# Input projections of a two-layer hybrid block: when weights, masks, decays and latents are queued

## Chip, core and metric

One core of a Trainium2 chip runs the whole program. The metric is the device time of one execution in microseconds (us); of several runs the median is taken. Five engines work side by side, each through its own list of instructions: TensorE (PE in the profile, with its weight loads as PEld), VectorE (DVE), ScalarE (ACT), GpSimd (POOL) and SyncE (SP), which in this kernel issues every DMA.

## What is computed

1024 latent tokens and 256 context tokens, each of 1024 features, pass through two layers. A layer normalises its input, projects it with one wide matrix into the columns of four head groups, runs each group, gates the results, and adds one output projection to the stream. The reference, cut to the projections and the parts that the change touches:

```python
def hybrid_layer(x, xc, ...):
    h = rmsnorm(x, norm_w) * (1 + scale[:, None]) + shift[:, None]
    hc = rmsnorm(xc, norm_w) * (1 + scale_c) + shift_c
    pl = split_cols(h @ w_in, IN_WIDTHS)        # A: cq, ckv, kr, gate; B, C: q, k, v, gate; D: z, xbc, dt
    pc = split_cols(hc @ w_in, IN_WIDTHS)
    ya_l, ya_c = mla_branch(...)                # A
    ...
    x = x + gate[:, None] * (jnp.concatenate([ya_l, yb_l, yc_l, yd_l], axis=-1) @ w_out)

def mla_keys(ckv, k_rope, kv_norm_w, w_kv_up, rope):
    kv = (rmsnorm(ckv, kv_norm_w) @ w_kv_up).reshape(bsz, n, MLA_HEADS, MLA_NOPE + MLA_V)
    ...
def mla_queries(cq, q_norm_w, w_q_up, rope):
    q = (rmsnorm(cq, q_norm_w) @ w_q_up).reshape(bsz, n, MLA_HEADS, MLA_NOPE + MLA_ROPE)
    ...
def ssd_scan(x, dt, bm, cm, a, init, with_output):
    a_cum = jnp.cumsum((dt * a).reshape(bsz, nc, SSD_CHUNK, nh), axis=2)   # the decays
    ...
```

Group A expands a latent of 128 features (`ckv`) to keys and values with `w_kv_up`, and one of 256 features (`cq`) to queries with `w_q_up`. Group D needs running sums of `dt * a` along the tokens, its decays. The second layer computes no output for context tokens.

## The kernel before

Every large product is made in float32r from a split of both factors into a high and a low half: three matmuls (L128, L129, L130: high by high, low weight by high, high by low) for each one of the reference. A weight tile arrives as `..._raw`, ACT casts it to the high half (L291) and DVE subtracts to get the low half (L292). This is `split_w`, L286. `split` (L282 to L284) does the same for an activation.

Buffers: `bg` is a ring of six tiles of 128x1024 words, for raw weights, splits on their way to DRAM (`qkhl`, `chl`, `ka`, `qa`) and latents on their way back (`c`); `tm` is a ring of eight. There are 35 general slots (`Slot`), taken and given back by hand in the program. Products of two kinds and all transpositions use the PSUM ring `TR` of two.

A layer first runs `in_proj`, then attention, then the output projection. `in_proj` is a list of 22 jobs, numbered 0 to 21. Job 0 makes the rotary key and the `dt` columns; after its last token group `after_decays` (L809) turns `dt` into decays: `Ssd.decays` is a chain of some thirty small steps on 128x80 tiles on DVE and ACT, three matmuls (two matmul instructions each in the profile) of `dta` with triangles of ones and with ones (`ps_cum`, L447 to L449), and more small steps on the result. Jobs 1 to 6 are the convolved columns, 7 to 12 gates, 13 and 14 `cq`, 15 `ckv`, 16 to 19 the token-major columns (`tm`) of groups B and C, and 20 and 21 the last two gates. A job fetches the next job's weights as it starts (`fetch`, L613).

The token-major jobs walk through tokens in pairs of tiles. The third step of a pair transposes (`ps_qkt`, L781) and sends the split result off (`qkhl`, L784, L785, L787). During jobs 17 to 19 each pair also takes two steps from the list `up`, made by `up_steps` (L832), which is group A's expansion: `begin` loads and splits both up-projection weights (`wqu`, 512 KB; `wku`, 256 KB); `load` and `load_q` fetch latents `c` (L846), which `norm` had stored; `keys` (`ps_k`), `values` (`ps_v`) and `queries` (`ps_q`) are products; `end` gives back slots. Three token groups are gone through (256 context tokens, then 512 and 512 latent ones); `AHEAD` says how many steps ahead of the end of the list so far a latent's load is put in. What is left of the list is run as job 20 starts (L1024 and after). At 2 steps a pair, layer 0 takes 30 steps inside the jobs and layer 1 takes 28.

The order of the work is set in two ways. In attention, PE's order is written out by hand (`manual_schedule`). Elsewhere the framework orders each engine's instructions as it builds the program: of those that its own timing takes to be ready, the one that stands first in the program. `soon` is a list of [delay, function]; `flush` (L795) calls, after each product group, what has come due, and `issue_after` keeps it behind that group's last matmul on PE. SP runs its DMAs in the order that it was given, and waits in front of one whose source or buffer isn't ready.

Attention's first pair of heads is prepared in the last two jobs. `first` is a list of steps (loads of `kk`, `qq`, scores `ps_s`, maxima `mp` at L1148, then `row`, the step that sends the row of maxima through `ps_m`, `ng` and a DMA to `ql`), filled with `idle` steps at its end (L1357). They are dealt out evenly over job 21's units (eight to each token group: 24 in layer 0 and 16 in layer 1).

Masks: `mask_r` (L152 to L158) holds 128x640 words of constants from DRAM, cast to float32r, and the identity; the scan of group D and the row step use it. The prologue (L1480 to L1529) loads and normalises the tokens and makes the modulation vectors.

Of the kernel before, what the change touches and what calls it, by code (L numbers as in the profile page):

```python
# [9 lines left out]
F32 = mybir.dt.float32  # L10
# [7 lines left out]
P = 128  # L18
# [16 lines left out]
POOL_TM = ()  # L35
UP_RATE = {17: 2, 18: 2, 19: 2}
SCALE_V = True
AHEAD = 1
SIDE0, SIDE1 = 2, 7
MAKE_AT = (1, 0)  # L40
THIRD = 3
# [16 lines left out]
def hybrid_block(ctx, tc, x, ctxt, c_t, w_fm, w_tm, w_mod, b_gate, p_col, p_row, w_qu, w_kvu, w_out,  # L58
# [49 lines left out]
    def free_all(slots):  # L108
        for s in slots:
            s.free()  # L110
# [13 lines left out]
    def ps(tag, name=None):  # L124
        return pp.tile([P, 512], F32, tag=tag, bufs=PS_BUFS[tag], name=name or f"ps_{tag}")
# [6 lines left out]
    def f32(ap):  # L132
        return ap.bitcast(F32)
# [15 lines left out]
    nc.sync.dma_start(out=base, in_=consts[:, 0:4 * P])  # L149
    ident, tri_u, tri_l, ones = [base[:, i * P:(i + 1) * P] for i in range(4)]  # L150
    rtm, cs = const([P, 8, 96]), const([P, 8, 32])
    mask_f = bg(name="mask_f")  # L152
    nc.sync.dma_start(out=mask_f[:, 0:5 * P], in_=consts[:, 4 * P:])
    mask_r = cp.tile([P, 6 * P], F32R, name="mask_r")
    nc.vector.tensor_copy(mask_r[:, 0:5 * P], mask_f[:, 0:5 * P])
    nc.vector.tensor_copy(mask_r[:, 5 * P:6 * P], ident)
    ident_r = mask_r[:, 5 * P:6 * P]
    st_r = [mask_r[:, 3 * P:4 * P], mask_r[:, 4 * P:5 * P]]  # L158
    mhalf = const([P, 16])
# [122 lines left out]
    def split(dst_hi, dst_lo, src, eng):  # L282
        nc.scalar.copy(dst_hi, src)  # L283
        eng.tensor_tensor(out=dst_lo, in0=src, in1=f32(dst_hi), op=ALU.subtract)  # L284

    def split_w(src, name, n=1024, eng=None):  # L286
        raw = bg((P, n), name=name + "_raw")
        nc.sync.dma_start(out=raw, in_=src)
        hi = Slot([P, n], F32R, name + "_hi")
        lo = Slot([P, n], F32R, name + "_lo")  # L290
        nc.scalar.copy(hi.t, raw)  # L291
        (eng or nc.vector).tensor_tensor(out=lo.t, in0=raw, in1=f32(hi.t), op=ALU.subtract)  # L292
        return hi, lo


# [117 lines left out]
    class Ssd:  # L413
# [5 lines left out]
        def decays(self, dt_raw):  # L419
# [24 lines left out]
            nc.vector.tensor_scalar(out=am, in0=am, scalar1=-1.0, scalar2=None, op0=ALU.mult)  # L444
            dta, acum, tot, dec = v, e1, e2, e3
            nc.vector.tensor_tensor(out=dta, in0=dt, in1=am.unsqueeze(1).to_broadcast(S80), op=ALU.mult)
            pcum = ps("TR", name="ps_cum")  # L447
            for i, tri in enumerate((tri_u, tri_l, ones)):
                mm(pcum[:, i * 80:i * 80 + 80], lhsT=tri, rhs=dta.rearrange("p t c -> p (t c)"), start=True, stop=True)  # L449
# [8 lines left out]
            nc.vector.tensor_tensor(out=dec, in0=dec, in1=dt, op=ALU.mult)  # L458
            self.dta = [acum.bitcast(F32R), dta.bitcast(F32R)]
            split(*self.dta, dta, nc.vector)  # L460
            self.dt, self.eac, self.etot, self.dec = dt, eac, etot, dec

        def alloc_y(self):
            (self.y, self.y_slots) = toks(["yd0", "yd1"], F32, self.need_ctx)
# [148 lines left out]
    def fetch(L, j):  # L613
        if j[0] == "tm":
            br, half = j[1]
            return [split_w(w_tm[L, br, half, :, u, :], f"wtm{u}", eng=nc.gpsimd if (br * 2 + half, u) in POOL_TM else None)
                    for u in range(2)]
        return [split_w(w_fm[L, j[1]], "wfm", eng=nc.gpsimd if j[1] in POOL_FM else None)]

    def products(ht, w, lo, n, tag="MX", each=lambda: None, ks=range(8), p=None):  # L620
        hh, hl, _ = ht
# [9 lines left out]
    def in_proj(L, ht, need_ctx, side, follow, both, begun, make_last):  # L631
# [177 lines left out]
        def after_decays():  # L809
            ssd.decays(dt_raw)  # L810
            free_all(dt_slots)

        def start_ssd():
            ssd.alloc_y()
# [17 lines left out]
        def up_steps():  # L832
            W = {}

            def begin():
                rf.append(load_rope_fm())
                W["q"] = split_w(w_qu[L], "wqu")
                raw = bg((P, 512), name="wku_raw")
                nc.sync.dma_start(out=raw, in_=w_kvu[L])
                W["ks"] = Slot([P, 2, 512], F32R, "wku")  # L840
                W["k"] = [W["ks"].t[:, e, :] for e in range(2)]
                split(*W["k"], raw, nc.vector)

            def latent(i, lo, n):
                r = bg((P, 2, 512), F32R, name="c")
# [3 lines left out]
            def load(lo, n):  # L849
                W["ck", lo] = latent(2, lo, n)  # L850
# [47 lines left out]
                W["ks"].free()  # L898
                rf.pop().free()

            r = [begin]
            for lo, n in GROUPS:
                r.insert(-AHEAD if lo else len(r), lambda lo=lo, n=n: load(lo, n))
                r += [lambda pair=pair, lo=lo, n=n: keys(pair, lo, n) for pair in range(2)]
                r += [lambda lo=lo, t=t: values(lo, t) for t in range(lo // P, (lo + n) // P, 2)]
                if lo >= NCTX or need_ctx:
                    r.insert(-1, lambda lo=lo, n=n: load_q(lo, n))
                    r += [lambda h=h, lo=lo, n=n: queries(h, lo, n) for h in range(4)]
            return r + [end]

# [127 lines left out]
    def attention(L, res, need_ctx, y, late, ahead):  # L1038
# [315 lines left out]
            return r + more, row  # L1354

        first, row = prep(*pairs[0])
        yield first + [row] + [idle] * 4  # L1357
        y_slots, tail = [], []
        order_of_pe = ExitStack()
        order_of_pe.enter_context(tc.manual_schedule(engines={mybir.EngineType.PE}))  # L1360
# [145 lines left out]
    for part in range(4):  # L1506
        if part == X_AT:
            load_x(range(6, NTILE))
        for i in range(4):
            if part and i >= AFTER:  # L1510
                for _ in range(-(-len(due) // (5 - i))):
                    due.pop(0)()
            mod_a[4 * part + i]()
        if part == X_AT:
            for t in range(6, NTILE):
                x_hat(xs[t].t)
            raw.update(early_ht(xs, GROUPS[2:]))
        if part % 2 == 0:
            add_half(ht)
        last, due = due, []  # L1520
        for g in ready:
            made(g, part)
        for f in last:
            f()
        if part == X_AT:
            for p in range(part + 1):
                made(GROUPS[2], p)
            ready.append(GROUPS[2])
    nc.sync.dma_start(out=rtm, in_=rope_tm)  # L1529
    for L in range(DEPTH):  # L1530
        need_ctx = L < DEPTH - 1
# [139 lines left out]
```

## Time and profile before

| | |
|---|---|
| median of 3 runs | 1789.11 us (1788.35 to 1792.08) |
| profiled execution, own time | 1792.62 us |
| its span (first to last instruction) | 1790.8 us |
| mean granted TensorE clock over the span | 0.990 |
| PE busy | 1713.7 us (96%) |
| DVE busy | 1137.0 us (63%) |
| POOL busy | 786.8 us (44%) |
| ACT busy | 731.3 us (41%) |
| DMA queue's share of 16 engines | 41.2% |

The profiled execution is one run of its own, 3.5 us above the median. Its rows are in microseconds from the span's start. "Granted clock" is the share of TensorE's full clock that the chip gave it in a stretch. In the timeline a bracket shows how long the engine had been idle before the instruction, and what released it; `x2` joins like instructions that follow one another. Matmuls overlap, so a start-to-start distance tells more than one's length.

### The profile page before, as it was taken

What the parts mean: (1) busy time and instruction counts of PE and PEld (TensorE: products, weight loads), DVE (VectorE), ACT (ScalarE), POOL (GpSimd) and SP (SyncE); (2) the same over time, 40 slices, a digit from 0 to 9 for tenths busy, and PEclk for the clock granted to TensorE, in tenths of its full rate; (3) what the DMA queues carried; (4) which work ended last, traced back from release to release, by engine and by line L of the source; (5) the groups of instructions that cost most, each with busy time, mean ns of one, the idle gap of its engine ahead of it and who ended that gap; (6) DMA issues with size and microseconds to landing.
All of it is one profiled execution on the core that took longest, in us unless ns stands there. A gap on an engine that the chain in (4) does not pass through costs nothing.

```text
span 1790.8 us, 27801 instructions
## 1 busy us (share of the span) xinstructions
PE 1713.7 (96%) x9658; PEld 1334.7 (75%) x9658; DVE 1137.0 (63%) x2291; ACT 731.3 (41%) x2049; POOL 786.8 (44%) x735
## 2 busy tenths in 40 slices
PE   6999999999989999999999899999999999999998
PEld 4677888889976566666787678888898655666686
DVE  6877864374347766577645797762743776657753
ACT  5433433333224555556424333343322355554531
POOL 2423642042325766656323234531332377666622
PEclk9999999999999999999999999999999999999999
DMA  9474323165556431431511344241568643131521
GB/s 321 143 239 150 116 101 127 60 203 192 194 157 173 115 98 31 114 102 63 194 59 42 111 151 148 75 144 60 182 196 249 176 131 91 32 92 60 160 69 56
DMA packets 130480, 231.61 MB, mean 129 GB/s; under 512 B 13826, under 2 KB 74628, under 8 KB 130340
## 3 DMA queue, kind: packets, MB, share of 16 engines
q1 hardware_dynamic: 130340, 229.84, 41.2%
q8 instruction: 76, 1.25, 0.3%
q14 instruction: 64, 0.52, 0.1%
HBM read 161.23 MB, written 68.45 MB: 128 GB/s over the span
## 4 chain that ended last, share of the span: by engine, by line
PE 52%; DVE 11%; DMA 4%; POOL 2%; issue 2%; ACT 2%; SPq 0%; POOLq 0%; DVEq 0%; ACTq 0%
PE ps_acc L1239 8%; PE ps_s L1144 4%; PE ps_fm L129 3%; PE ps_fm L130 3%; PE ps_fm L128 3%; PE ps_o L130 3%; PE ps_o L128 3%; PE ps_o L129 3%; PE ps_st L1227 3%; PE ps_st L1230 2%; PE ps_st L1222 2%; DVE mp L1148 2%; PE ps_st L1223 2%; PE ps_st L1224 2%; PE ps_tm L128 1%
## 5 line engine op out<-in xcount | busy, mean ns | idle before, releaser
L1254 POOL TENSOR_TENSOR ac<-ac,P 128x512 f32<-128x512 f32 (+3 forms) x248 | 308.2, 1261 | 130.6 <-ACT P L1231 95.4
L1231 ACT ACTIVATE P<-ps_st 128x512 f32<-128x512 f32 (+3 forms) x456 | 243.3, 553 | 214.3 <-PE ps_st L1230 98.5
L1148 DVE TENSOR_REDUCE mp<-ps_s 128x1 f32<-128x512 f32 (+3 forms) x428 | 259.2, 656 | 100.8 <-PE ps_s L1144 96.3
L128 PE MATMUL ps_fm<-hh,wfm_hi 128*128 128x512 f32 x576 | 234.2, 407 | 2.6 <-DVE kb L660 1.9
L130 PE MATMUL ps_fm<-hl,wfm_hi 128*128 128x512 f32 x576 | 232.2, 403 | 2.2 <-POOL hl L405 1.0
L129 PE MATMUL ps_fm<-hh,wfm_lo 128*128 128x512 f32 x576 | 230.1, 399 | 0.0
L128 PE MATMUL ps_tm<-wtm_hi,hh 128*128 128x256 f32 x512 | 147.1, 287 | 1.6 <-ACT ka L283 1.6
L129 PE MATMUL ps_tm<-wtm_hi,hl 128*128 128x256 f32 x512 | 146.2, 286 | 0.0
L130 PE MATMUL ps_tm<-wtm_lo,hh 128*128 128x256 f32 x512 | 146.2, 286 | 0.0
L1254 DVE TENSOR_TENSOR ac<-ac,P 128x512 f32<-128x512 f32 (+3 forms) x88 | 98.7, 1121 | 53.5 <-ACT P L1231 19.5
L130 PEld LDWEIGHTS ps_fm<-hl,wfm_hi 128*128 128x128 f32 x576 | 109.5, 190 | 28.9 <-POOL hl L405 4.5
L128 PEld LDWEIGHTS ps_fm<-hh,wfm_hi 128*128 128x128 f32 x576 | 109.8, 191 | 27.5 <-issue 5.1
L129 PEld LDWEIGHTS ps_fm<-hh,wfm_lo 128*128 128x128 f32 x576 | 109.7, 190 | 21.4 <-issue 2.5
L1248 POOL TENSOR_TENSOR ac<-P 128x1024 f32<-128x1024 f32 (+1 forms) x30 | 65.9, 2198 | 117.1 <-ACT P L1231 99.7
L128 PE MATMUL ps_o<-wo_hi,yh 128*128 128x512 f32 x288 | 112.6, 392 | 1.4 <-ACT yh L1403 1.3
L129 PE MATMUL ps_o<-wo_hi,yl 128*128 128x512 f32 x288 | 112.1, 390 | 1.4 <-DVE yl L1404 1.4
L130 PE MATMUL ps_o<-wo_lo,yh 128*128 128x512 f32 x288 | 112.0, 390 | 0.0
L128 PEld LDWEIGHTS ps_tm<-wtm_hi,hh 128*128 128x128 f32 x512 | 99.1, 194 | 3.9 <-ACT ka L283 2.0
L130 PEld LDWEIGHTS ps_tm<-wtm_lo,hh 128*128 128x128 f32 x512 | 99.3, 194 | 0.6 <-issue 0.4
L129 PEld LDWEIGHTS ps_tm<-wtm_hi,hl 128*128 128x128 f32 x512 | 99.2, 194 | 0.5
L1448 POOL TENSOR_TENSOR xres<-xres,dl 128x512 f32<-128x512 f32 x32 | 42.4, 1326 | 95.6 <-DVE dl L1447 92.4
L1239 PE MATMUL ps_acc<-P,vt 128*64 128x512 f32 (+3 forms) x416 | 82.5, 525 | 0.0
(342 smaller groups left out, 4123.9 us busy)
## 6 DMA issues: line engine op xcount, KB each, us to landing
wfm_raw<-in_w_fm_dram SPq DMA_DIRECT2D x36, 512.0 KB
wm<-in_w_mod_dram SPq DMA_DIRECT2D x64, 256.0 KB
d_q<-qkhl SPq DMA_DIRECT2D x18, 512.0 KB
wm<-in_w_mod_dram SPq DMA_DIRECT2D x16, 512.0 KB
d_gate<-th SPq DMA_DIRECT2D x32, 256.0 KB
wtm_raw<-in_w_tm_dram SPq DMA_DIRECT2D x16, 512.0 KB
qq<-d_q SPq DMA_DIRECT2D x32, 256.0 KB
wo_raw<-in_w_out_dram SPq DMA_DIRECT2D x16, 512.0 KB
```

Source lines behind the costliest of these rows:

```text
L128: mm(o, lhsT=lh, rhs=rh, start=first, stop=False)
L129: mm(o, lhsT=ll, rhs=rh, start=False, stop=False)
L130: return mm(o, lhsT=lh, rhs=rl, start=False, stop=last)
L1144: mm(o, lhsT=qh(lo + t * P, P, 0, km), rhs=kh(k0, w, 0, km), start=True, stop=mo is None)
L1148: nc.vector.tensor_reduce(out=dst, in_=p[:, :nu * w].rearrange("p (u k) -> p u k", u=nu), axis=AX.X, op=ALU.max)
L1222: mm(st, lhsT=k(k0, 96), rhs=q(q0, 96), start=True, stop=False)
L1227: mm(st, lhsT=k(k0, 128), rhs=q(q0, 128), start=True, stop=False)
L1231: nc.scalar.activation(out=pts[:, h, :w], in_=st, func=AF.Exp, scale=op["scale"])
L1239: mm(acc[h * 64:h * 64 + 64, c0:c0 + w], lhsT=op["v"].tile(kb)[:, v0:v0 + 64], rhs=pts[:, h, :w], start=(bi == 0), stop=(bi == len(blocks) ...
L1248: nc.gpsimd.tensor_tensor(out=s[:, :, :n], in0=sums[0][:, :, :n], in1=pts[:, :, :n], op=ALU.add)
L1254: eng.tensor_tensor(out=s[:, h, c0:c0 + w], in0=s[:, h, c0:c0 + w], in1=pts[:, h, :w], op=ALU.add)
L1448: (nc.vector if t == ts[-1] else nc.gpsimd).tensor_tensor(out=xt.t[:, js], in0=xt.t[:, js], in1=d, op=ALU.add)
```

## The change

- `mask_r`'s load and its two casts move from the top of the program to behind the prologue's loops, ahead of the load of `rope_tm`.
- `split_w` gets `roomy`: with it, and with more than four slots free, the raw tile is a slot of its own and not a tile of the ring. It is set for the weights of the last gate (`FM_GATE + 5`, job 21).
- `Ssd.decays` is cut in two. The three matmuls and all that comes behind them are now `cumulate`, put on `soon` with a delay of 1.
- `up_steps`: `begin` loads the rotary table and `wku` alone. `wqu` has a step `begin_q`, three from the end of the list as it stands when the first queries are added. Two empty steps follow the first latent's load. With `AHEAD` at 2 the other two latent loads go in one step earlier. The list grows from 31 to 34 steps in layer 0 and from 26 to 29 in layer 1.
- The first attention pair gets eight `idle` steps and not four.

```diff
--- before.py
+++ after.py
@@ -35,7 +35,7 @@
 POOL_TM = ()
 UP_RATE = {17: 2, 18: 2, 19: 2}
 SCALE_V = True
-AHEAD = 1
+AHEAD = 2
 SIDE0, SIDE1 = 2, 7
 MAKE_AT = (1, 0)
 THIRD = 3
@@ -149,11 +149,7 @@
     nc.sync.dma_start(out=base, in_=consts[:, 0:4 * P])
     ident, tri_u, tri_l, ones = [base[:, i * P:(i + 1) * P] for i in range(4)]
     rtm, cs = const([P, 8, 96]), const([P, 8, 32])
-    mask_f = bg(name="mask_f")
-    nc.sync.dma_start(out=mask_f[:, 0:5 * P], in_=consts[:, 4 * P:])
     mask_r = cp.tile([P, 6 * P], F32R, name="mask_r")
-    nc.vector.tensor_copy(mask_r[:, 0:5 * P], mask_f[:, 0:5 * P])
-    nc.vector.tensor_copy(mask_r[:, 5 * P:6 * P], ident)
     ident_r = mask_r[:, 5 * P:6 * P]
     st_r = [mask_r[:, 3 * P:4 * P], mask_r[:, 4 * P:5 * P]]
     mhalf = const([P, 16])
@@ -283,13 +279,16 @@
         nc.scalar.copy(dst_hi, src)
         eng.tensor_tensor(out=dst_lo, in0=src, in1=f32(dst_hi), op=ALU.subtract)
 
-    def split_w(src, name, n=1024, eng=None):
-        raw = bg((P, n), name=name + "_raw")
+    def split_w(src, name, n=1024, eng=None, roomy=False):
+        own = Slot([P, n], F32, name + "_raw") if roomy and len(free_slots) > 4 else None
+        raw = own.t if own else bg((P, n), name=name + "_raw")
         nc.sync.dma_start(out=raw, in_=src)
         hi = Slot([P, n], F32R, name + "_hi")
         lo = Slot([P, n], F32R, name + "_lo")
         nc.scalar.copy(hi.t, raw)
         (eng or nc.vector).tensor_tensor(out=lo.t, in0=raw, in1=f32(hi.t), op=ALU.subtract)
+        if own:
+            own.free()
         return hi, lo
 
 
@@ -444,6 +443,10 @@
             nc.vector.tensor_scalar(out=am, in0=am, scalar1=-1.0, scalar2=None, op0=ALU.mult)
             dta, acum, tot, dec = v, e1, e2, e3
             nc.vector.tensor_tensor(out=dta, in0=dt, in1=am.unsqueeze(1).to_broadcast(S80), op=ALU.mult)
+            self.dt, self.tmp = dt, (dta, acum, tot, dec, eac, etot)
+
+        def cumulate(self):
+            dt, (dta, acum, tot, dec, eac, etot) = self.dt, self.tmp
             pcum = ps("TR", name="ps_cum")
             for i, tri in enumerate((tri_u, tri_l, ones)):
                 mm(pcum[:, i * 80:i * 80 + 80], lhsT=tri, rhs=dta.rearrange("p t c -> p (t c)"), start=True, stop=True)
@@ -458,7 +461,7 @@
             nc.vector.tensor_tensor(out=dec, in0=dec, in1=dt, op=ALU.mult)
             self.dta = [acum.bitcast(F32R), dta.bitcast(F32R)]
             split(*self.dta, dta, nc.vector)
-            self.dt, self.eac, self.etot, self.dec = dt, eac, etot, dec
+            self.eac, self.etot, self.dec = eac, etot, dec
 
         def alloc_y(self):
             (self.y, self.y_slots) = toks(["yd0", "yd1"], F32, self.need_ctx)
@@ -615,7 +618,7 @@
             br, half = j[1]
             return [split_w(w_tm[L, br, half, :, u, :], f"wtm{u}", eng=nc.gpsimd if (br * 2 + half, u) in POOL_TM else None)
                     for u in range(2)]
-        return [split_w(w_fm[L, j[1]], "wfm", eng=nc.gpsimd if j[1] in POOL_FM else None)]
+        return [split_w(w_fm[L, j[1]], "wfm", eng=nc.gpsimd if j[1] in POOL_FM else None, roomy=j[1] == FM_GATE + 5)]
 
     def products(ht, w, lo, n, tag="MX", each=lambda: None, ks=range(8), p=None):
         hh, hl, _ = ht
@@ -809,6 +812,7 @@
         def after_decays():
             ssd.decays(dt_raw)
             free_all(dt_slots)
+            soon.append([1, ssd.cumulate])
 
         def start_ssd():
             ssd.alloc_y()
@@ -834,12 +838,14 @@
 
             def begin():
                 rf.append(load_rope_fm())
-                W["q"] = split_w(w_qu[L], "wqu")
                 raw = bg((P, 512), name="wku_raw")
                 nc.sync.dma_start(out=raw, in_=w_kvu[L])
                 W["ks"] = Slot([P, 2, 512], F32R, "wku")
                 W["k"] = [W["ks"].t[:, e, :] for e in range(2)]
                 split(*W["k"], raw, nc.vector)
+
+            def begin_q():
+                W["q"] = split_w(w_qu[L], "wqu")
 
             def latent(i, lo, n):
                 r = bg((P, 2, 512), F32R, name="c")
@@ -898,13 +904,18 @@
                 W["ks"].free()
                 rf.pop().free()
 
-            r = [begin]
+            r, seen = [begin], []
             for lo, n in GROUPS:
                 r.insert(-AHEAD if lo else len(r), lambda lo=lo, n=n: load(lo, n))
+                if not lo:
+                    r += [lambda: None] * 2
                 r += [lambda pair=pair, lo=lo, n=n: keys(pair, lo, n) for pair in range(2)]
                 r += [lambda lo=lo, t=t: values(lo, t) for t in range(lo // P, (lo + n) // P, 2)]
                 if lo >= NCTX or need_ctx:
                     r.insert(-1, lambda lo=lo, n=n: load_q(lo, n))
+                    if "q" not in seen:
+                        seen.append("q")
+                        r.insert(-3, begin_q)
                     r += [lambda h=h, lo=lo, n=n: queries(h, lo, n) for h in range(4)]
             return r + [end]
 
@@ -1354,7 +1365,7 @@
             return r + more, row
 
         first, row = prep(*pairs[0])
-        yield first + [row] + [idle] * 4
+        yield first + [row] + [idle] * 8
         y_slots, tail = [], []
         order_of_pe = ExitStack()
         order_of_pe.enter_context(tc.manual_schedule(engines={mybir.EngineType.PE}))
@@ -1526,6 +1537,10 @@
             for p in range(part + 1):
                 made(GROUPS[2], p)
             ready.append(GROUPS[2])
+    mask_f = bg(name="mask_f")
+    nc.sync.dma_start(out=mask_f[:, 0:5 * P], in_=consts[:, 4 * P:])
+    nc.vector.tensor_copy(mask_r[:, 0:5 * P], mask_f[:, 0:5 * P])
+    nc.vector.tensor_copy(mask_r[:, 5 * P:6 * P], ident)
     nc.sync.dma_start(out=rtm, in_=rope_tm)
     for L in range(DEPTH):
         need_ctx = L < DEPTH - 1
```

## Rows read from the trace of the kernel before

**Rows 1.** The page: the span, and TensorE's busy time with its share.

```profile
span 1790.8 us, 27801 instructions
...
PE 1713.7 (96%) x9658; PEld 1334.7 (75%) x9658; DVE 1137.0 (63%) x2291; ACT 731.3 (41%) x2049; POOL 786.8 (44%) x735
```

**Rows 2.** PE's waits: instruction <- releaser: us in total, times, longest.

```profile
PE ps_st L1230 <- DMA ql<-ng: 5.0, 3, 2.2
```

**Rows 3.** Table by windows: length, busy time (instructions) per engine, clock, DMA share, GB/s.

```profile
402.00:406.00 4.00, 3.73 (x19) 3.74 (x20) 1.68 (x5) 1.73 (x6) 0.00 (x0) 0.57 0.29 98
515.00:522.00 7.00, 6.62 (x18) 5.38 (x19) 1.26 (x3) 0.00 (x0) 0.00 (x0) 0.53 0.94 297
545.00:550.00 5.00, 5.00 (x18) 4.16 (x18) 3.23 (x5) 2.39 (x4) 0.13 (x1) 0.66 0.74 195
1023.00:1031.00 8.00, 7.26 (x30) 4.22 (x30) 1.47 (x8) 1.33 (x6) 0.00 (x0) 0.57 0.34 117
1300.00:1304.00 4.00, 4.00 (x23) 3.94 (x22) 1.72 (x3) 0.63 (x2) 0.00 (x0) 0.60 0.75 272
```

**Rows 4.** Timeline, start: start, us, engine, line, operation [idle before <- releaser].

```profile
6.52 0.49 DVE L155 CAST mask_r<-mask_f 128x640 fp32r<-128x640 f32 x1
...
6.93 0.15 DVE L350 TENSOR_SCALAR xrs<-xrs 128x1 f32<-128x1 f32 x1
...
8.55 1.76 PE L371 MATMUL ps_xt<-con,x 128*128 128x128 f32 x7 [8.55 <-DVE x L356]
```

**Rows 5.** Table by windows, the first 25 us.

```profile
0.00:25.00 25.00, 12.44 (x81) 9.32 (x81) 13.94 (x38) 15.19 (x39) 3.51 (x10) 1.00 0.95 340
```

**Rows 6.** Timeline of PE: ps_cum in layer 0; in layer 1, a row ahead.

```profile
93.27 0.79 PE L449 MATMUL ps_cum<-s,con 128*128 128x80 f32 x6
...
1020.87 0.39 PE L128 MATMUL ps_fm<-hh,wfm_hi 128*128 128x512 f32 x1
...
1023.74 1.54 PE L449 MATMUL ps_cum<-s,con 128*128 128x80 f32 x6 [2.48 <-DVE s L446]
```

**Rows 7.** Timelines of DVE and PE at the first keys of layer 0.

```profile
400.05 1.22 DVE L292 TENSOR_TENSOR wqu_lo<-wqu_raw,wqu_hi 128x1024 fp32r<-128x1024 f32 x1
...
401.52 0.68 DVE L284 TENSOR_TENSOR wku<-wku_raw,wku 128x512 fp32r<-128x512 f32 x1
...
402.26 0.58 PE L129 MATMUL ps_k<-c,wku 128*128 128x256 f32 x1 [3.29 <-DVE wku L284]
```

**Rows 8.** Timeline of PE: the transposition that closes a token pair, twice running.

```profile
387.03 0.60 PE L781 MATMUL ps_qkt<-con,qkv 128*128 128x128 f32 x4
...
393.23 0.60 PE L781 MATMUL ps_qkt<-con,qkv 128*128 128x128 f32 x4
```

**Rows 9.** Timelines, layer 1: query weights (SP, ACT, DVE), first keys and latent (PE).

```profile
1276.05 1.09 SPq L288 DMA_DIRECT2D wqu_raw<-in_w_qu_dram  x1
...
1282.97 1.05 ACT L291 CAST wqu_hi<-wqu_raw 128x1024 fp32r<-128x1024 f32 x1 [1.52 <-DMA wqu_raw<-in_w_qu_dram]
...
1286.99 1.21 DVE L292 TENSOR_TENSOR wqu_lo<-wqu_raw,wqu_hi 128x1024 fp32r<-128x1024 f32 x1
...
1288.86 0.39 PE L129 MATMUL ps_k<-c,wku 128*128 128x256 f32 x1 [1.48 <-DVE wku L284]
...
1298.48 0.47 PE L128 MATMUL ps_k<-c,wku 128*128 128x512 f32 x1 [2.96 <-DMA c<-d_c]
```

**Rows 10.** Timelines of SP and PE: the last gate's weights in layer 0.

```profile
505.80 0.58 SPq L288 DMA_DIRECT2D wfm_raw<-in_w_fm_dram  x1
...
514.13 0.38 PE L128 MATMUL ps_fm<-hh_cx,wfm_hi 128*128 128x256 f32 x1 [2.67 <-ACT wfm_hi L291]
...
515.38 0.58 PE L129 MATMUL ps_fm<-hh_cx,wfm_lo 128*128 128x256 f32 x1 [0.88 <-DVE wfm_lo L292]
```

**Rows 11.** Timelines of SP and PE: last key store, first `ql`.

```profile
518.38 0.54 SPq L787 DMA_DIRECT2D d_k<-qkhl  x1
...
544.77 0.50 PE L1230 MATMUL ps_st<-ql,kk_cx 65*128 65x512 f32 x1 [2.15 <-DMA ql<-ng]
```

## The prediction

> **What bounds the kernel now.** I read the busy shares first: TensorE (PE) is busy 96% of the span [rows 1], so 1790.8 − 1713.7 = 77 us are all that waiting costs directly, and no edit here removes a product. What can be had is idle time of PE, and what follows it. So I went next to PE's waits, which name the releaser of each idle stretch. The reader is to see that they are many and small: the three waits for the maximum row `ql`, for example, make 5.0 us together, none over 2.2 [rows 2]. The table by windows then shows the second half of the price. After a stall PE's granted clock is well under full: 0.57 over 402–406, 0.53 over 515–522, 0.66 over 545–550, 0.57 over 1023–1031, 0.60 over 1300–1304 [rows 3], that is, near the lower of its two levels (1.2 of 2.4 GHz) for most of the stretch. What that costs is length times (1 − clock): 1.7, 3.3, 1.7, 3.4 and 1.6 us. A stall of 2 to 3 us is thus worth 4 to 7. Last I read the timeline around each stall that an edit touches, to see which wait ends last there.
>
> All sums are made on the profiled execution, 1792.6 us; it stands 3.5 above the median of the timed runs, 1789.1, and the forecast is moved by that at the end.
>
> **Masks later.** Before, the mask's 320 KB are loaded and cast by VectorE (DVE) in the first microseconds. The first cast runs 6.52 to 7.01 and DVE's next step, the row statistic at L350, starts right then, at 6.93; PE's first transposition starts at 8.55, waiting on DVE [rows 4]. The cast thus delays DVE by at most 0.49 us, and the transfer, at the 340 GB/s of the first 25 us where the DMA engines are 0.95 busy [rows 5], by 0.33 MB / 340 GB/s = 1.0 us. PE's start depends on several loads at once, so I take 0.7, from −0.5 (the casts, now behind the prologue on DVE, hold up one of its later steps by their 0.49) to 1.5 (both prices whole). On the sync queue (SP) the load moves past the prologue's weight loads; its users stand far behind, in the projections' scan, so its later arrival costs nothing as long as it lands ahead of them.
>
> **Decays' products later.** In layer 0 the six matmuls of `ps_cum` show no idle time before them; in layer 1 PE waits 2.48 us for DVE at 1023.74 [rows 6], and with the 3.4 us of clock behind it that place costs 5.9. The edit queues the products behind the first group of the next job. But the row at 1020.87 belongs to that job's second group and already runs ahead of `ps_cum` [rows 6]: the products stand later than the new earliest place, because the framework orders PE by its own estimate of readiness, and that estimate hardly changes. I take 0, the value that this row is nearest to; bounds 0 to 5.9. The DVE and ScalarE (ACT) steps after the products move with them and have a whole conv job as cover.
>
> **Keys' weights first.** In layer 0 DVE makes `wqu_lo` (1.22 us) ahead of `wku`'s low half (0.68, ready at 402.20), while PE waits 3.29 us until 402.26 in the first key product [rows 7]. The edit takes the query weights out of `begin`, which frees those 1.22 us and SP's issue of 512 KB ahead of `wku_raw`, and adds two empty steps, one token pair, before the keys: 6.20 us by the two transpositions one pair apart [rows 8]. PE wanted `wku` at 398.97; a pair later, at 405.2, it is 3.0 us old. So the wait goes, 3.29 + 1.7 = 5.0. In layer 1 the same wait is 1.48 [rows 9], with the same margin: together 6.5, bounds 3 (a wait on another input replaces half) to 6.5. What is next: the key products move behind another pair's products, which keep PE busy meanwhile.
>
> **Latents one step earlier.** In layer 1 PE waits 2.96 us at 1298.48 for the latent load `c` [rows 9]; with 1.6 of clock, 4.6. `AHEAD` 2 puts the load one more step, half a pair or 3.1 us, ahead of its use, just over the wait. I take 4.0; bounds 0 (the load's buffer comes free no earlier) to 4.6.
>
> **Last weights in a slot, row earlier.** In layer 0 the load of the last gate's weights is issued at 505.80, and PE then waits 2.67 us for the high half and 0.88 for the low half [rows 10]; with 3.3 of clock, 6.9. Before, the raw tile waits for one of six ring buffers; by my count of the code six general slots are free at that point in layer 0 and seven in layer 1, over the four that the new condition asks for, so the load no longer waits for the ring. The same ACT and DVE queue heads (the casts of these weights) stand before the last key split, whose store is issued only at 518.38; the loads and maxima of the first attention pair follow from it, and at 544.77 PE waits 2.15 us for `ql` [rows 11], 3.9 with its 1.7 of clock. Eight empty steps instead of four put the row step at unit 16 of 24 instead of 20, and in layer 1 at the same place as before, so there nothing moves. I take all of the 6.9 and 1.6 of the 3.9: 8.5, bounds 5 (the idle 3.55 and half the clock) to 10.8. The raw tile holds its slot for some 10 us (505.80 to 515.38); nothing else asks for one there.
>
> **What is added.** The query weights now start four steps, two pairs or 12.4 us, before the first query. In layer 1 today their chain runs from the issue at 1276.05 over the cast at 1282.97 to the end of `wqu_lo` at 1288.20: 12.2 us [rows 9]. The cover is just enough, and behind the waiting query products PE's later pairs are queued. The longer list (31 steps to 34 in layer 0, 26 to 29 in layer 1, against 30 and 28 taken in the loop) leaves three queries and the clean-up of layer 0 to the start of the gate that precedes attention. No row of before shows these waits. The nearest are the waits of 1.48 and 2.96 us in the same place [rows 9], with 1.6 each 3.1 and 4.6. I take 4 lost, about one of them; bounds 0 and 8, one in each layer.
>
> **Sum.** 0.7 + 0 + 6.5 + 4.0 + 8.5 − 4 = 15.7 gained. On the profiled execution that is 1776.9, on the median's scale 1773.4. All favourable ends: 1.5 + 5.9 + 6.5 + 4.6 + 10.8 = 29.3, or 1760. All unfavourable: −0.5 + 0 + 3 + 0 + 5 − 8 = −0.5, or 1790.
>
> **Rivals.** (a) *The order hardly changes.* The framework's estimate orders PE outside attention, so the change may not do what it says; if it puts the keys and latents back where they were, only the freed DVE step (1.22 of the 3.29, plus its share), the slot and the start stay: 6 to 8 us, 1782. For it speaks `ps_cum`, which stands late already [rows 6]; against it, the empty steps are real steps of the list. (b) *Every wait goes* and the chain of 12.2 us is covered: 29 us, 1760. Against it, its cover is only 0.2 us. (c) *New waits take all back*: two stalls of the 4.6 kind in each layer, 18 us, 1789 to 1791. (d) *Slower: the ring becomes the bound.* Six ring buffers hold latents (now one step longer), key and query splits, raw weights. If the query weights get theirs one pair (6.2 us) late, the first query waits about 6.0 plus 3.3 of clock, 9.3 in each layer, 18.6; two pairs late it is 12.2 + 3.3 = 15.5 a layer. The remaining gain is 19.7 without the 4 already charged, so it decides from 9.9 a layer; at 14 a layer, between the two, 8.3 are lost and the time is 1797. For it: a ring wait is what I read into the late issue at 505.80 [rows 10]. Against it: one raw tile leaves the ring, and `wqu_raw` no longer stands in it beside `wku_raw`. (e) *The loads behind the moved weights arrive late.* 512 KB of query weights now go into the one SP queue ahead of the next latents; at 340 GB/s [rows 5] they need 1.5 us, and a query or key product that waits for it pays 3.2 with its clock, 6.4 in two layers: 1780. In today's order the load of the same weights took 6.92 us from issue to cast [rows 9], so transfers do wait for others there.
> The Trainium skill, page "DMA: Bandwidth & Descriptors", section "Queues, rings and completion order", says that each DMA engine consumes the descriptors of one queue in ring order; by that rule (e) follows whenever the moved load is still under way. The 6.92 us of the trace agree with it but don't prove it.
>
> **Chances and range.** Forecast, 1768 to 1778: 0.38. (a) 0.22, (b) 0.12, (c) 0.12, (d) 0.08, (e) 0.08. A measurement of this kernel tells about 0.2%, 3.6 us, from no change; under 1785.5 is faster. So faster is 0.38 + 0.22 + 0.12 + 0.08 = 0.80, the same 0.12, slower 0.08. The range 1760 to 1787 leaves out (d), most of (c) and the tail of (b).
>
> **What the changed profile would show.** Right: no PE wait for `wku` near 405 and 1292, none for `c` near 1300, none for `wfm_hi` near 510; granted clock near 1 in those windows; `ps_st` released at 533 to 541 with a shorter wait for `ql`. The wait before `ps_cum` in layer 1 stays (my 0) or goes (5.9 more). Wrong: a new wait of the first `ps_q` for `wqu_lo` or its latents, ACT idle on the `wqu_raw` load, or SP waiting in front of that load. The forecast fails if those new waits exceed 8 us, or if the stretch of layer 0 from 500 to 545 shortens by under 5.

## The result, and the profile after

The changed kernel takes 1779.95 us (median of 4 runs, 1777.71 to 1781.63) and the kernel before beside it 1790.59 (1788.35 to 1794.05): a ratio of 0.9946, 95% interval 0.9931 to 0.9960, or 10.6 us at the medians. The forecast was 1773. The profiled execution of after is one of 1777.71 us, 2.2 under its median, while that of before lies 2.0 above the median of these runs, so the two traces differ by more than the medians: 14.9 us of span.

The page of after (span; busy time and share of each engine):

```profile
span 1775.9 us, 27832 instructions
...
PE 1703.8 (96%) x9658; PEld 1327.8 (75%) x9658; DVE 1137.4 (64%) x2291; ACT 731.7 (41%) x2049; POOL 787.5 (44%) x735
```

Beside [rows 1], PE does the same 9658 instructions and is busy for 9.9 us less: the same products ran at the higher clock for longer (mean granted clock 0.994 and not 0.990, so 10.7 us lost to it over the span and not 17.9). Idle time fell only from 77.1 to 72.1.

Where the time went is seen best by numbering PE's instructions in both traces. The order differs a little near the edits, but equal numbers mean about equal work done. The lead is after less before; a step is its change since the line above, and a negative one is time gained:

| PE instruction | before, us | after, us | lead | what lies in the step |
|---|---|---|---|---|
| 339 | 69.0 | 69.0 | 0.0 | the start |
| 2347 | 391.1 | 391.7 | +0.6 | first jobs of layer 0 |
| 2473 | 411.1 | 406.7 | −4.4 | first keys of layer 0: −5.0 |
| 3085 | 491.4 | 483.7 | −7.7 | rest of the token-major jobs: −3.3 |
| 3364 | 554.2 | 536.2 | −17.9 | last gates and first row of maxima: −10.2 |
| 5477 | 997.1 | 979.2 | −17.9 | attention, output, start of layer 1 |
| 5794 | 1057.6 | 1036.6 | −21.1 | `ps_cum` in layer 1: −3.2 |
| 7350 | 1318.6 | 1292.4 | −26.2 | keys and latents of layer 1: −5.1 |
| 7606 | 1352.0 | 1330.8 | −21.2 | third group's keys in layer 1: +5.0 |
| 7956 | 1419.3 | 1404.8 | −14.5 | last token pair of layer 1, gates: +6.7 |
| 9653 | 1781.8 | 1767.0 | −14.9 | to the end |

So 26.2 us were gained, near the favourable end of the forecast's sum, and 11.7 were lost again in two places of layer 1. PE's waits in after name them (instruction <- releaser: us in total, times, longest):

```profile
PE ps_qkt L784 <- POOL qkv L739: 5.5, 2, 5.2
...
PE ps_tm L128 <- DVE qkv L728: 2.6, 1, 2.6
PE ps_cum L452 <- DVE s L445: 2.2, 1, 2.2
PE ps_st L1241 <- issue: 2.1, 1, 2.1
...
PE ps_k L129 <- DVE wku L280: 2.1, 1, 2.1
```

Against [rows 2]: in layer 0 the first `ps_st` waits 0.26 us for `ql` in place of 2.15; in layer 1 the same step still waits 2.1, now put down to "issue". The waits for `c` and `wfm_hi` [rows 9, 10] are gone. Of the first two lines shown, the one stood at 1.9 us in before and the other not at all. The table by windows of after (columns as in [rows 3]) shows the second half of the price:

```profile
398.00:402.00 4.00, 4.00 (x36) 4.00 (x35) 3.34 (x10) 1.69 (x5) 1.01 (x1) 1.00 0.50 168
502.00:510.00 8.00, 8.00 (x40) 6.75 (x39) 2.49 (x4) 2.64 (x6) 6.08 (x5) 1.00 0.89 218
...
1004.00:1012.00 8.00, 6.16 (x40) 4.55 (x41) 4.22 (x14) 2.56 (x9) 0.00 (x0) 1.00 0.21 61
...
1328.00:1334.00 6.00, 5.61 (x34) 5.61 (x35) 2.26 (x7) 1.11 (x3) 0.87 (x2) 0.72 0.77 249
1364.00:1371.00 7.00, 6.24 (x17) 5.00 (x18) 1.86 (x4) 2.07 (x5) 1.94 (x2) 0.55 0.85 241
```

The stretches of layer 0 in [rows 3] that answer to the first two lines run at full clock now; two new ones in layer 1, at 0.72 and 0.55, cost 6.0 × 0.28 = 1.7 and 7.0 × 0.45 = 3.2 us.

The chain behind the first loss, from the timelines of after (layer 1, third group's keys):

```profile
1324.04 0.70 DVE L896 TENSOR_TENSOR qb<-ps_q,rfm 32x512 f32<-32x512 f32 x1
...
1324.88 1.27 POOL L897 TENSOR_TENSOR qf<-qf,qb 32x512 f32<-32x512 f32 x1 [3.73 <-DVE qb L896]
...
1326.18 0.62 ACT L279 CAST qa<-qf 96x512 fp32r<-96x512 f32 x1 [3.77 <-POOL qf L897]
1326.71 0.57 ACT L279 CAST ka<-ps_k 128x512 fp32r<-128x512 f32 x1
...
1327.32 0.69 DVE L280 TENSOR_TENSOR ka<-ps_k,ka 128x512 fp32r<-128x512 f32 x1 [2.58 <-ACT ka L279]
1327.92 0.41 DVE L728 COPY qkv<-ps_tm 128x256 f32<-128x256 f32 x1
...
1328.39 0.38 PE L128 MATMUL ps_tm<-wtm_hi,hh 128*128 128x256 f32 x1 [2.57 <-DVE qkv L728]
```

The reader is to see one query's steps going round three engines (DVE, POOL, ACT). ACT waits 3.77 us for POOL at the head of its queue, the cast of the new key (`ka`) stands behind it, DVE's low half behind that, the copy of the token pair (`qkv`) behind that, and PE's next token-major product needs the buffer that this copy frees. The second loss, at the last token pair of layer 1:

```profile
1358.50 0.69 DVE L896 TENSOR_TENSOR qb<-ps_q,rfm 32x512 f32<-32x512 f32 x1 [2.29 <-DMA d_v<-v]
...
1359.34 1.25 POOL L897 TENSOR_TENSOR qf<-qf,qb 32x512 f32<-32x512 f32 x1 [4.46 <-DVE qb L896]
...
1361.32 1.26 POOL L280 TENSOR_TENSOR qa<-qf,qa 96x512 fp32r<-96x512 f32 x1 [0.73 <-ACT qa L279]
1362.65 1.25 POOL L897 TENSOR_TENSOR qf<-qf,qb 32x512 f32<-32x512 f32 x1
1363.98 0.72 POOL L739 TENSOR_TENSOR qkv<-ra,rb 128x256 f32<-128x256 f32 x1
...
1364.76 0.69 PE L784 MATMUL ps_qkt<-con,qkv 128*128 128x128 f32 x2 [5.19 <-POOL qkv L739]
```

Three query steps of 1.25 us and a wait for ACT between them stand on POOL in front of the pair's own step (`qkv`), and PE stands in front of `ps_qkt` for 5.19 us.

### The profile page after: what moved, and what is told of

It is laid out like the page before. It is cut to its first block, busy times and chain, and to the rows that moved or that the text cites. A ratio compares the mean times of both kernels' runs of the same rounds, so it can differ in the third digit from the quotient of the medians.

```text
span 1775.9 us, 27832 instructions
## 1 busy us (share of the span) xinstructions
PE 1703.8 (96%) x9658; PEld 1327.8 (75%) x9658; DVE 1137.4 (64%) x2291; ACT 731.7 (41%) x2049; POOL 787.5 (44%) x735
## 3 DMA queue, kind: packets, MB, share of 16 engines
q8 instruction: 76, 1.25, 0.3%
## 4 chain that ended last, share of the span: by engine, by line
PE 75%; DVE 12%; DMA 4%; issue 3%; POOL 3%; ACT 2%; SPq 1%; POOLq 0%; DVEq 0%; ACTq 0%
PE ps_acc L1250 9%; PE ps_fm L128 7%; PE ps_fm L130 7%; PE ps_fm L129 7%; PE ps_s L1155 4%; PE ps_o L129 3%; PE ps_o L130 3%; PE ps_o L128 3%; PE ps_tm L128 3%; PE ps_tm L130 3%; PE ps_tm L129 3%; PE ps_st L1238 3%; PE ps_st L1241 3%; PE ps_st L1233 2%; PE ps_st L1235 2%
```

## The experiments

Ratios are against the kernel before on the same chip; after itself has 0.9946 (0.9931 to 0.9960). Timed runs of one kernel spread by 4 to 9 us, so most of what follows is read from the traces. Theory 1 held that each part of the change does what its place in the code suggests, and that the losses in layer 1 come from the early last weights (the first) and the longer list (the second). The first four kernels undo one part each.

**The empty steps undone, both layers.**

```diff
-                if not lo:
-                    r += [lambda: None] * 2
```

> The changed kernel without the two empty steps in the list of up-projection steps; all else as changed. Theory 1 (the stall of 5.2 us before ps_qkt near 1364 in layer 1, with its half clock some 8 us, comes from the last two queries standing in the last token pair because the list is longer): the stall goes, layer 1 gains 6 to 9, layer 0 gives back 0 to 5 at the first keys near 400; total 1771 to 1779, with a gap between the traces that opens near 1360. Rival (that stall comes from the early last weights and the crowded transfers, not from the list): the stall stays, total 1780 to 1785 as the keys of layer 0 wait again.

1777.2 us, ratio 0.9941 (0.9922 to 0.9959): the same as after, but for two opposite reasons. Its trace has waits in layer 0 that after has not, and in layer 1 only half of the second one (timeline of PE):

```profile
400.70 0.39 PE L129 MATMUL ps_k<-c,wku 128*128 128x256 f32 x1 [1.52 <-DVE wku L280]
...
504.29 0.69 PE L784 MATMUL ps_qkt<-con,qkv 128*128 128x128 f32 x2 [2.58 <-POOL qkv L739]
...
1366.70 0.44 PE L784 MATMUL ps_qkt<-con,qkv 128*128 128x128 f32 x2 [2.73 <-POOL qkv L739]
```

The wait near 1328 is gone altogether. Against after, this trace loses 6.1 us between PE instructions 2347 and 3364 of layer 0 and gains 9.4 between 7350 and 7956 of layer 1. The empty steps earn in layer 0 about what they cost in layer 1.

**The slot for the last weights undone.**

```diff
-        return [split_w(w_fm[L, j[1]], ..., roomy=j[1] == FM_GATE + 5)]
+        return [split_w(w_fm[L, j[1]], ..., roomy=False)]
```

> The changed kernel with the last gate's raw weights back in the ring of six, in both layers. Theory 1 (the early casts of the last weights hold up ScalarE in layer 1 from 1310 to 1321 and cause the 2.6 us wait of ps_tm near 1328): layer 0 loses 6 to 8 near 500 to 520, layer 1 gains 4 to 5 near 1328; total 1780 to 1784. Rival (the wait of ps_tm comes from the queries and keys alone): layer 1 gains nothing, total 1786 to 1788.

1780.4 us, ratio 0.9956 (0.9939 to 0.9973). The time lies in theory 1's range, but neither of its two parts happened, and the rival's range is missed: both expectations fall. In layer 0 the weights come in time through the ring too: their load is issued at 492.20, ahead of the next store of query splits (`d_qa`, 496.12), and cast at 496.54, and PE doesn't wait for them; only a wait for `ql` of 1.76 at 529.47 is left. In layer 1 the wait of `ps_tm` stays (2.58, at 1330.85), so the early casts are not its cause, and the other one falls to 0.44, while 2.75 us come up behind it in front of the row step (`ps_m`); the 2.28 us for `ql` that follow were 2.15 in after.

**The slot in layer 0 alone.**

```diff
-roomy=j[1] == FM_GATE + 5
+roomy=L == 0 and j[1] == FM_GATE + 5
```

> The changed kernel with the slot for the last weights used in layer 0 alone; layer 1 takes the ring. Theory 1 (the early casts in layer 1 cause the wait near 1328): the 4.7 us of layer 1 come back and layer 0 keeps its gain: 1774 to 1777. Rival (they are harmless): 1779 to 1781, with the wait of ps_tm still there.

1777.6 us, ratio 0.9945 (0.9929 to 0.9962). Layer 1 shows the same as in the run above. Timeline of PE:

```profile
1327.44 0.38 PE L128 MATMUL ps_tm<-wtm_hi,hh 128*128 128x256 f32 x1 [2.58 <-DVE qkv L728]
...
1362.68 0.44 PE L784 MATMUL ps_qkt<-con,qkv 128*128 128x128 f32 x2 [0.43 <-POOL qkv L739]
...
1386.69 0.38 PE L1188 MATMUL ps_m<-con,mr 128*8 128x128 f32 x1 [2.75 <-DVE mr L1184]
...
1389.30 0.76 PE L1241 MATMUL ps_st<-ql,kk_cx 65*128 65x512 f32 x1 [2.23 <-DMA ql<-ng]
```

What it gains before the row step it partly gives back there: against after, 6.0 us in layer 1 up to that step and 3.4 lost again by the first `ps_acc`. The time lies between the two ranges; that the wait near 1328 is still there is the rival's sign.

**The decays' products called at once again.**

```diff
             ssd.decays(dt_raw)
+            ssd.cumulate()
             free_all(dt_slots)
-            soon.append([1, ssd.cumulate])
```

> The changed kernel with the decays' three matmuls and what follows them called at once again, as before. Theory 1 (queueing them later is worth the 3.2 us that layer 1 gained near 1020 and the 1.0 of layer 0 near 90): total 1783 to 1785, and ps_cum in layer 1 waits 2 to 3 us with a clock of some 0.57 behind it. Rival, my prediction (the place on PE does not change, the gain came from elsewhere): 1779 to 1781.

1781.4 us, ratio 0.9961 (0.9946 to 0.9976), which overlaps that of after. On PE the six products of layer 1 only change places with four neighbours, and their wait is 2.48 us where after has 2.16 [rows 6]. That part is worth 0.3 us of idle time; nearly all of the 3.2 us of the table is a difference of the clock behind nearly the same wait (last section).

From these, theory 2: in layer 1 the empty steps make the wait near 1328, and the early last weights that of `ps_qkt` near 1364.

**Empty steps and slot in layer 0 alone.**

```diff
-                if not lo:
+                if not lo and need_ctx:
                     r += [lambda: None] * 2
...
-roomy=j[1] == FM_GATE + 5
+roomy=L == 0 and j[1] == FM_GATE + 5
```

> The changed kernel with the two empty steps and the slot for the last weights in layer 0 alone. Theory 2, from the first four runs (in layer 1 the empty steps make the wait of ps_tm near 1328, the early last weights the wait of ps_qkt near 1364; behind both stands the row step): both waits go, 9 to 10 us, and 3 to 4 come back as a wait of the row step (ps_m and ql) near 1385; total 1772 to 1775. Rival (one of them takes the other's place, as the empty steps and the weights both only decide what collides): 1776 to 1779.

1768.7 us, ratio 0.9891 (0.9876 to 0.9905): 19 us under the kernel before and, with the run below, the fastest of all, with an interval clear of that of after. PE's waits in layer 1 of this kernel, from the timeline:

```profile
1265.24 0.39 PE L129 MATMUL ps_k<-c,wku 128*128 128x256 f32 x1 [1.49 <-DVE wku L280]
...
1353.63 0.69 PE L784 MATMUL ps_qkt<-con,qkv 128*128 128x128 f32 x2 [2.69 <-POOL qkv L739]
...
1383.34 0.47 PE L1241 MATMUL ps_st<-ql,kk_cx 65*128 65x512 f32 x1 [2.14 <-issue]
```

The wait near 1328 is gone, the one of `ps_qkt` is halved, and the keys wait no longer than with the empty steps (1.49 against 2.1). The time lies under both ranges: `ps_qkt` keeps 2.69 us though the last weights are no longer early, so the second half of theory 2 fails, and the row step waits no longer than in after. What is left of theory 2 is that in layer 1 the empty steps are what costs.

**Empty steps in layer 0 alone, the slot in both.**

```diff
-                if not lo:
+                if not lo and need_ctx:
                     r += [lambda: None] * 2
```

> The changed kernel with the two empty steps in layer 0 alone; the slot for the last weights stays in both layers. Theory 2 (in layer 1 the empty steps are what costs: with the list two steps shorter the last queries leave the last pair, and the early last weights then meet nothing): the waits near 1328 and 1364 fall from 2.6 and 5.2 us to nothing and under 3, total 1768 to 1772, as with both edits in layer 0 alone. Rival (the early last weights are a cost of their own in layer 1): the wait of ps_qkt stays over 4 us, total 1773 to 1777.

1770.3 us, ratio 0.9887 (0.9869 to 0.9904), the same as the run above; `ps_qkt` too (timeline of PE):

```profile
1357.87 0.44 PE L784 MATMUL ps_qkt<-con,qkv 128*128 128x128 f32 x2 [2.73 <-POOL qkv L739]
```

So the two empty steps cost layer 1 some 10 us by the times, 7 to 9 by the three traces without them, and the slot there is neither gain nor loss once they are gone. In these traces 2 to 4 of the 11.7 us stay lost; the list is still one step longer there than in before. And beside the first run, which differs in layer 0 alone, the empty steps earn 9.7 us in layer 0 by the ratios.

**Query weights loaded in the first step again.**

```diff
             def begin():
                 rf.append(load_rope_fm())
+                begin_q()
...
-                        r.insert(-3, begin_q)
```

> The changed kernel with the query weights loaded and split in the first step again, ahead of the key weights; the empty steps stay. Theory 1 (the keys' wait in layer 0 went because wqu's low half no longer stands before wku's on VectorE): a wait of ps_k for wku of 1 to 3 us in layer 0 near 400, and the last weights of layer 0 late again near 510; total 1783 to 1787. Rival (the empty steps alone cover it, since 6.2 us are more than the 3.3 that were missing): no wait over 1 us near 400, 1779 to 1781.

1783.0 us, ratio 0.9972 (0.9959 to 0.9984). In layer 0 the keys wait again, and `ps_qkt` waits 2.33 us at 508.36 (timeline of PE):

```profile
408.27 0.58 PE L129 MATMUL ps_k<-c,wku 128*128 128x256 f32 x1 [2.14 <-DVE wku L280]
```

That is theory 1 for the keys; the last weights, which it wanted late again, are in time. The list is also a step shorter here, since `begin_q` leaves it. The empty steps alone don't cover the keys; the order of the weights alone doesn't either (first run, 1.52). It takes both.

**Latents one step ahead, as before.**

```diff
-AHEAD = 2
+AHEAD = 1
```

> The changed kernel with latents loaded one step ahead again. Theory 1 (loading earlier removed the wait of 3.0 us for c in layer 1): that wait comes back in layer 1 between 1270 and 1330, 3 to 5 us, total 1782 to 1785. Rival (the two empty steps alone are enough): no wait for c over 1 us, 1779 to 1781.

1777.9 us, ratio 0.9945 (0.9928 to 0.9962). Waits for `c` come up (timeline of PE):

```profile
474.98 0.52 PE L128 MATMUL ps_k<-c,wku 128*128 128x512 f32 x1 [1.83 <-DMA c<-d_c]
...
1322.58 0.50 PE L128 MATMUL ps_k<-c,wku 128*128 128x512 f32 x1 [2.36 <-DMA c<-d_c]
```

They aren't the wait of before [rows 9]: that one stood at the keys of the second token group, and these stand at the third. The second group's load goes out 4.4 us ahead of its keys in before; in this run it goes out 7.4 us ahead, and PE doesn't wait (timelines of SP and PE; the first row is of before, the others of this run):

```profile
1294.04 0.58 SPq L846 DMA_DIRECT2D c<-d_c  x1
...
1273.81 0.57 SPq L852 DMA_DIRECT2D c<-d_c  x1
...
1281.19 0.48 PE L128 MATMUL ps_k<-c,wku 128*128 128x512 f32 x1
```

So the extra step spares the changed kernel two waits that before did not have, and isn't what removed the one it had. Nor does the total move, since what follows in layer 1 then waits less (`ps_qkt` 3.00 and not 5.19).

**Four empty steps in the first attention pair.**

```diff
-        yield first + [row] + [idle] * 8
+        yield first + [row] + [idle] * 4
```

> The changed kernel with four empty steps and not eight in the first attention pair. Theory 1 (the earlier row step is what removed the wait for ql in layer 0): a wait of ps_st for ql of about 2 us comes back near 528 with 1.7 to 3.4 of clock, total 3 to 5 above the changed kernel, 1782 to 1785. Rival (the row came earlier because the last weights no longer hold up the key split; the step's place is of no use): less than 1 us, 1779 to 1781.

1779.1 us, ratio 0.9953 (0.9937 to 0.9970). The wait for `ql` at 529.31 is 0.96 us, in after 0.26: a gain of 0.7, nearly as the rival has it.

**Masks at the top again.**

```diff
+    mask_f = bg(name="mask_f")
+    nc.sync.dma_start(out=mask_f[:, 0:5 * P], in_=consts[:, 4 * P:])
     mask_r = cp.tile([P, 6 * P], F32R, name="mask_r")
+    nc.vector.tensor_copy(mask_r[:, 0:5 * P], mask_f[:, 0:5 * P])
+    nc.vector.tensor_copy(mask_r[:, 5 * P:6 * P], ident)
```

> The changed kernel with the masks loaded and cast at the top again. Theory 1 (they delay the first normalisation on VectorE by half a microsecond and the token loads by up to 1.0): PE's first matmul 0.3 to 1.5 us later and the same at 70 us; total 1780 to 1782. Rival (the start is bound by the token loads alone): no step at 70 us in the traces, 1779 to 1781; the timed medians cannot tell the two apart, the trace at 30 to 70 us can.

1782.7 us, ratio 0.9956 (0.9942 to 0.9969). PE starts at 8.70, in after at 8.16. At 70 us this trace is 1.6 behind, nearly all of it a longer stretch at the lower clock, such as some kernels with the masks late show as well. Half a microsecond can be put down to the masks; whether there is more isn't settled.

**Three steps a pair in job 18**, on top of the kernel with both edits in layer 0.

```diff
-UP_RATE = {17: 2, 18: 2, 19: 2}
+UP_RATE = {17: 2, 18: 3, 19: 2}
```

> The kernel with the empty steps and the slot in layer 0 alone, and three steps of the list a pair in job 18 (two before). Theory 2 (what is left in layer 1, 2.7 us of ps_qkt behind the last queries' GpSimd steps, comes from queries beside the last pairs): with the list done some two pairs earlier that wait falls under 1 us with its 1.7 of clock; total 1764 to 1768. Rival (the same steps, packed more tightly, collide in job 18 instead): new waits of ps_tm or ps_k in job 18 of 2 to 5 us, total 1769 to 1775.

1775.9 us, ratio 0.9926 (0.9904 to 0.9949). The wait of `ps_qkt` leaves layer 1, as theory 2 has it, but its twin appears in layer 0, and smaller ones come up in layer 1 (1.68 for `c` and 1.39 for the copy of a pair):

```profile
499.35 0.69 PE L784 MATMUL ps_qkt<-con,qkv 128*128 128x128 f32 x2 [5.14 <-POOL qkv L739]
```

In layer 0 the faster rate brings in the queries that had been left for job 20, and, by the count of the list, they now stand beside the last pair. The time lies just over the rival's range. The rate would have to be set for each layer; that wasn't run.

**Ten buffers in the ring of `qb` and `v`.**

```diff
-ring("tm", 8, 512)
+ring("tm", 10, 512)
```

> The changed kernel with ten buffers in the ring of 128x512 tiles, eight before; PE's order is the same but for a few rows. Theory 2 in its detail (in layer 1 VectorE's step qb near 1358 waits 2.3 us for a buffer of that ring, which the store of v must give back, and this wait is the first link of the 5.2 us of ps_qkt): that wait goes, the wait of ps_qkt falls to 3.0 or less with 3.4 of clock and not 6.8, total 1774 to 1778. Rival (the wait of ps_qkt comes from GpSimd's three query steps of 1.25 us in front of qkv, whatever the ring): it stays at 4.5 or more, total 1779 to 1781.

1778.9 us, ratio 0.9939 (0.9917 to 0.9961). The detail falls. DVE's wait is still there, and `ps_qkt` still waits for POOL:

```profile
1363.10 0.70 DVE L896 TENSOR_TENSOR qb<-ps_q,rfm 32x512 f32<-32x512 f32 x1 [2.38 <-DMA d_v<-v]
...
1368.66 0.69 PE L784 MATMUL ps_qkt<-con,qkv 128*128 128x128 f32 x2 [4.60 <-POOL qkv L739]
```

So the ring's size isn't what holds `qb`; why it waits for that store stays open. What is shown is where the query steps stand, not why the first of them is late.

## Why the prediction was right in sign and range, and where it was off

- **Masks**, 0.7 taken: 0.4 at PE's first product (8.55 to 8.16), nothing left at 69 us, 0.5 in the run that undid it. Small, as said.
- **Decays**, 0 taken: right, and for the reason given: the place on PE hardly changes, and undoing it moves the wait by 0.3. The rest of the 3.2 us at that place is the clock's.
- **Keys in layer 0**, 5.0 taken: 5.0 measured, no wait, clock 1.00 at 398 to 402. Two runs show that the order of the weights and the empty steps are both needed.
- **Keys in layer 1**, 1.5 taken: failed. The empty steps did not move the first key product there: it is PE instruction 7141 before and 7127 after, and 7127 too in the four kernels without empty steps there; with the query weights back in the first step it is 7141 again. So taking those weights out let the framework put the keys 14 places earlier, and they still wait, 2.07 us for `wku`. The framework's order, which I had as rival (a), decided here and not the empty steps.
- **Latents**, 4.0 taken: the wait of 2.96 went and 5.1 us were gained there, the absent clock loss included, but not by the step that was to earn it. With `AHEAD` at 1 that wait stays away, and undoing the step leaves the ratio at 0.9945. It stays away, too, without the empty steps and with the query weights in the first step, so no single edit is shown as its cause.
- **Last weights and row**, 8.5 taken, 10.2 measured, but the step that named the cause failed. The slot is worth only 1.5 us in layer 0 (the wait for `ql` without it), the eight empty steps 0.7. The weights came in time through the old ring once the rest had changed. What held the load up in before was something else (below the list).
- **What is added**, 4 taken (0 to 8): mis-sized, and the largest error. It cost 11.7 us, all in layer 1, over the bound of 8. I had looked for the new waits at the first query and its weights; there PE doesn't wait at all (`wqu` is cast at 1290.28 after ACT waited 0.15 us for it, and the first query follows at 1299). I did not price what a list three steps longer puts beside the **last** pair, though the count stood in the text: 29 steps with 28 taken means that the last two queries fall into the last pair; with 26 they were done a pair earlier. The count fits layer 0 as well: two queries fall into its last pair in the first run and in the one with the query weights in the first step, where `ps_qkt` waits 2.58 and 2.33 us, and one in after, where it doesn't wait. Nor did I ask, layer by layer, whether the empty steps were needed: layer 1 lacked 1.48 us and got 6.2.

Of the last weights I had read a wait for the ring into the issue at 505.80 [rows 10]; the SP queue of before shows none. The load goes out as the DMA ahead of it ends, and what SP waited for stands further ahead: two stores of query splits, `d_qa`, for which POOL's `qa` came late (waits of SP from 484 to 512, then timeline):

```profile
SPq L894 <- POOL qa L284: 8.3, 2, 5.6
...
496.88 3.96 SPq L894 DMA_DIRECT2D d_qa<-qa  x2
...
504.98 0.78 SPq L1051 DMA_DIRECT2D kk<-d_k  x1
```

Without the slot the changed kernel has the load ahead of the next such store (492.20 against 496.12). Which part of the change moved it, and whether the framework's estimate of the ring had put it behind them, isn't shown.

Rival (e) didn't occur: in after no product waits for latents behind the moved weights. The Trainium skill's rule on ring order ("DMA: Bandwidth & Descriptors", section "Queues, rings and completion order") is neither confirmed nor denied by that, since the next latents were issued at 1290.14, 6.5 us behind the 512 KB of query weights (1283.62), whose cast began at 1290.28.

By the table the gains were 26.2 us where I had 19.7 (15.7 + 4). The 6.5 more are, net, the 3.2 at `ps_cum`, nearly all clock, and 3.3 along the token-major jobs of layer 0 that I didn't count; in before PE waited 1.60 us there for `ka`, in after it doesn't. The loss was 11.7 where I had 4. Two errors of 6.5 and 7.7 us nearly cancelled, so it is partly luck that the total fell inside the range.

## What to carry to other kernels

An edit to a list of steps that is dealt out over a loop moves everything behind it: count what then falls into the last turns, and in each layer separately, before pricing the wait that the edit was read from. A stall on late weights needn't be cured where it shows; ask first what held them up. The same two empty steps earned 6 to 10 us in layer 0, where the keys lacked 3.3, and cost some 10 in layer 1, where they lacked 1.5 and the steps didn't move them. And a load that is issued late hasn't always waited for its own buffer: look at what the queue stood in front of before it.

## What the runs showed of the hardware

The clock behind a stall isn't a fixed price. `ps_cum` in layer 1 waits 2.1 to 2.5 us in every trace, and the granted clock over the 8 us around it was 0.57 in before [rows 3], 0.79 in the kernel without the empty steps and 1.00 in after:

```profile
1016.00:1024.00 8.00, 7.89 (x41) 6.04 (x42) 2.89 (x7) 2.71 (x9) 0.00 (x0) 0.79 0.08 19
```

That is 3.4, 1.7 or 0 us for nearly the same wait: after it PE fell to 1.2 of its 2.4 GHz for longer, for less long, or not at all. Nor is it the edit that decides: nine traces that queue `ps_cum` later show 0.79 there and three show 1.00, behind waits of 2.15 to 2.17 us; the one that undoes it shows 0.79 as well. Pricing each stall with its clock, as the prediction did, fits the keys of layer 0 (5.0 us taken, 5.0 measured), but is uncertain by that much for a single stall.
